# One instruction for both PSUM banks of an output block, other banks for the MLP's products, and later splits of the unmixed inner blocks

## The chip, the cores and the metric

The kernel runs on one core of a Trainium2 chip. The metric is the device time of one execution in microseconds (us), measured over several runs. TensorE (PE in the profile; PEld is its weight load) multiplies, VectorE (DVE), ScalarE (ACT) and GpSimd (POOL) compute elementwise, and SyncE (SP) issues most DMAs. PE writes only into PSUM, which has eight banks; each engine takes its instructions in order and waits on semaphores that other engines raise.

## The reference

One layer of a hybrid decoder on 544 tokens (512 of a prompt, 8 x 4 of samples), all in f32:

- `proj = rmsnorm(x) @ w_in`, cut into gated linear attention (GLA) and dilated attention with ALiBi; both are computed for prompt and samples, the samples with a key/value cache and a recurrent state.
- `x = x + concat(gla_part, att_part) @ w_out`
- `h = rmsnorm(x, ffn_norm_w)`; `x + square(relu(h @ w_up)) @ w_down`, with `w_up` 2048 x 8192 and `w_down` 8192 x 2048; then the final RMSNorm.
- Outputs are the two `y`, the prompt's and samples' keys and values, and the GLA states.

## The kernel before, in words

Everything lies transposed: 128 features on the partitions, 544 tokens along the free axis, in two halves of 272 (`HALF`). An f32 product is made of three: weights and activations are split into a high and a low part, and wh*xh, wh*xl and wl*xh are summed in PSUM. ACT copies the high part of a weight quad (128 x 512, `whP` in the MLP), DVE subtracts it from the weight to get the low part (`wlP`). Three buffers of each rotate (`NWH = 3`), and the splits are recorded ahead: before unit s of the MLP runs, units up to s+2 are split (`run`, line 1299, by `prep_to`). All engine calls go through one helper (line 95), so the profile's rows all carry L95 and are told apart by tile names.

**Projections** (to about 937 us of the profile). 48 blocks of `w_in` and then `w_out` are multiplied block by block over 24 x 2 matmuls a half; `mpair` (line 310) hands out the bank pairs 0,1 and 2,3 in turn, bank 0 and 2 for token half 0, bank 1 and 3 for half 1. `evac_in` (409), `evac_att` (1158) and `evac_wo` (1164) take the two halves out with one DVE instruction each. Attention and GLA steps are put between, by a planner that adds up estimated costs per engine, with banks 4 to 7.

**MLP, up** (about 937 to 1630 us). Pairs p = 0..31 of output blocks are computed with a seven-product scheme (Strassen's in Winograd's form): products P1 to P7 over sums of weight quads (`add_w`, DVE) and of activation halves. A unit is one product over four contraction blocks, 12 matmuls of 128 x 272. `ua`, `ub`, `uc` (1317) say which bank each product uses; `up_after` takes products out and forms the hidden block pair, `hidden_ops` squares, scales and stores it. Such small steps wait in the list `post`, of which `run` takes one before each unit. For p = 28 to 31 (g = 7) the hidden blocks are not mixed into sums: they are multiplied by the squared row norm (`mul`) and split into high and low (`spill_two`: an ACT copy, a DVE subtraction, two stores).

**MLP, down** (about 1630 to 2222 us). For g = 0..6 and p = 0..7, seven units in the order of `D_ORDER`. Each product is added into the accumulator tiles by one DVE instruction of 128 x 272 as soon as its unit ends (`down_after`; for g = 0 the first writes of four of the seven are ACT copies). Even p use banks 0 to 3, odd p banks 4 to 7 (lines 1510, 1516 and 1566):

```python
dbank = {"P1": (0, True), "P2": (0, False), "P5": (1, True), "P4": (1, False), "P7": (2, True), "P3": (2, False),
         "P6": (3, True)}
ps = halfb(bank[4 * (p % 2) + dbank[k][0]])
D_ORDER = ("P1", "P5", "P2", "P6", "P7", "P4", "P3")
```

**Last part** (2222 us to the end). The eighth group of `w_down` is multiplied directly, 16 blocks for each token half, two units a block, in the banks `LB` (1626); then the final norm.

Order within an engine is the order of the program text. Waits between engines are placed by the framework, which follows who wrote and read a tile.

Of the kernel before, what the change touches and what calls it, by code (L numbers as in the profile page):

```python
# [6 lines left out]
F32 = mybir.dt.float32  # L7
# [3 lines left out]
OP = mybir.AluOpType  # L11
AX = mybir.AxisListType

D = 2048
NTOK = 544
SEQ = 512
HALF = 272
# [105 lines left out]
def _body(ctx, nc, tc, A):  # L123
# [3 lines left out]
    psum = ctx.enter_context(tc.tile_pool(name="ps", bufs=1, space=bass.MemoryType.PSUM))  # L127
    ctx.enter_context(tc.manual_schedule())

    bank = [psum.tile([128, 512], F32, name=f"bank{i}") for i in range(8)]  # L130
    mbank = bank[:4]
    bfree = list(bank[4:])

# [60 lines left out]
    V, S, G, P = (Engine(e, k, clk) for e, k in ((nc.vector, "V"), (nc.scalar, "S"), (nc.gpsimd, "G"), (nc.tensor, "P")))  # L194
# [45 lines left out]
    i = 6  # L240
# [4 lines left out]

    def half(t, hf):
        return t[:, hf * HALF:(hf + 1) * HALF]

    def wops(i):
        return (lambda c: whm[i, c // 4][:, c % 4, :]), (lambda c: wlm[i, c // 4][:, c % 4, :])  # L250
# [8 lines left out]
    post = []  # L259
# [127 lines left out]
    r_bc = alloc()  # L387
# [9 lines left out]
    def rms_r(dst, srcs, n, banks):  # L397
        t, y = alloc(), alloc()
        for hf in range(2):
            for i, s in enumerate(srcs):  # L400
                P.matmul(banks[hf][:, :HALF], ones, half(s, hf), start=i == 0, stop=i == len(srcs) - 1)
        for hf in range(2):
            rsq(half(dst, hf), banks[hf][:, :HALF], n, half(t, hf), half(y, hf))
        rel(t, y)
# [4 lines left out]
    def evac_in(idx, pb):  # L409
        kind, h, _ = order[idx]  # L410
        t = alloc()
        sc = QSCALE if kind in ("q", "gq") else 1.0
        for hf in range(2):
            V.scalar_tensor_tensor(half(t, hf), pb[hf][:, :HALF], sc, half(r_bc, hf), op0=OP.mult, op1=OP.mult)
        B[kind, h] = t
        ready[kind, h] = slot[0]
        if kind in ("q", "k", "v"):
            j = "qkv".index(kind)
            S.activation(KVS[h // 4][:, j * 128 + (h % 4) * 32:j * 128 + (h % 4) * 32 + 32], t[:, SEQ:], AF.Copy)
        if kind in ("k", "v"):  # L420
            dst = A["kT" if kind == "k" else "vT"][h]
            defer(1, lambda: nc.sync.dma_start(dst, t))
# [625 lines left out]
    for idx in range(3, len(order)):  # L1048
# [3 lines left out]
        if kind == "gq" and h == 0:  # L1052
            begin()
            pb = mpair()
# [11 lines left out]
        pb = (b0, b1) if idx == 3 else mpair()  # L1066
# [90 lines left out]

    def evac_att(nb):
        def f(pb):
            for hf in range(2):  # L1160
                V.tensor_add(half(xr[nb], hf), pb[hf][:, :HALF], half(xr[nb], hf))
        return f

    def evac_wo(nb):
        def f(pb):
            t = xr[nb]
            for hf in range(2):
                V.tensor_add(half(t, hf), pb[hf][:, :HALF], half(t, hf))
            sq = {}

            def scaled():
                a = xa[nb] = alloc()
                S.activation(a, t, AF.Copy, scale=nw[:, 16 + nb:17 + nb])

            def squared():
                q = sq["q"] = ss2 if nb == 0 else alloc()
                S.activation(q, t, AF.Square)
                nc.gpsimd.dma_start(A["x2s"][nb], t)
                rel(t)

            def summed():
                if nb:
                    V.tensor_add(ss2, ss2, sq["q"])
                    rel(sq["q"])
            post.extend([scaled, squared, summed])
            j = nb - 8
            if j >= 0:
                post.extend(lambda f=f: f(j) for f in (up_b2, up_b1, up_ta, up_ta2, up_tb, up_tb2))
        return f
# [124 lines left out]
            unit_no[0] += 1  # L1314


    ua = [bank[0], bank[1]]
    ub, uc = [bank[2], bank[6]], [bank[3], bank[7]]
    tmp = {}
    hid = {}  # L1320

    def halfb(b):
        return b[:, :HALF]
# [2 lines left out]

    def r2_calc():
        r2sq = rr["sq"] = alloc()
        rms_r(r2sq, [ss2], D, (bank[4], bank[5]))
        V.tensor_mul(r2sq, r2sq, r2sq)  # L1330
        rel(ss2)

# [12 lines left out]
    def hidden_ops(p):  # L1345
        g, j = p // 4, p % 4
        a1, a2 = hid.pop((p, 0)), hid.pop((p, 1))
        if g == 7:
            def put(i, a):
                spill_two(a, A["hl"][2 * j + i], 0)  # L1350
                rel(a)
            post.extend([lambda: V.tensor_mul(a1, a1, rr["sq"]), lambda: V.tensor_mul(a2, a2, rr["sq"]),
                         lambda: put(0, a1), lambda: put(1, a2)])
            return
        dst = A["hs"][g, j]
        m = {}

        def mix_a():
            ta = m["a"] = alloc()
            V.tensor_sub(half(ta, 0), half(a1, 1), half(a1, 0))  # L1360
            V.tensor_sub(half(ta, 1), half(a1, 1), half(a2, 1))

        def first():
            t = alloc(R32)
            put_x(half(t, 0), half(t, 1), half(a1, 0))
            rel(a1)
            spill(t, dst[6])

        def mix_b():
            tb = m["b"] = alloc()  # L1370
            V.tensor_sub(half(tb, 0), half(a2, 1), half(m["a"], 0))
            V.tensor_sub(half(tb, 1), half(tb, 0), half(a2, 0))

        def put_a():
            spill_two(m["a"], dst, 2)
            rel(m["a"])

        def put_2():
            spill_two(a2, dst, 0)
            rel(a2)  # L1380

        def put_b():
            spill_two(m["b"], dst, 4)
            rel(m["b"])

        post.extend([mix_a, first, mix_b, put_a, put_2, put_b])
# [236 lines left out]
        return [kept, second, third]  # L1623

    perm = (0, 2, 4, 6, 1, 3, 5, 7)
    LB = [bank[i] for i in (0, 1, 2, 3)]
    fin = {}
    XL = {}

    def evac_last(hf, nb, pb):  # L1630
        t = half(acc[nb], hf)
        V.tensor_add(t, halfb(pb), t)
        if nb == 15:
            square(hf, nb)
# [50 lines left out]
    def last_mm(hf, nb, q):  # L1685
        def f():
            xs_ = XL.setdefault("x", [ah[n] for n in perm])
            key = ("L", hf, nb, q)
            ps = halfb(LB[nb % 4])
            for w, o in ((whm, 0), (whm, 1), (wlm, 0)):  # L1690
                for c in range(4):
                    P.matmul(ps, w[key][:, c, :], half(xs_[4 * q + c][o], hf), start=q == 0 and w is whm and o == 0 and c == 0,
                             stop=q == 1 and w is wlm and c == 3)
        return f
# [16 lines left out]
    for hf in range(2):  # L1711
        for nb in range(16):
            raw_seq.append((("l", hf, nb), A["wdn"][7, nb]))
            for q in range(2):
                raw_last["l", hf, nb] = len(units)

                def prep(hf=hf, nb=nb, q=q):
                    split_last(("L", hf, nb, q), mraw["l", hf, nb][:, 4 * q:4 * q + 4, :])
                add_unit(Unit(("L", hf, nb, q), prep, last_mm(hf, nb, q), before=last_before(hf, nb, q),
                              after=(lambda hf=hf, nb=nb: evac_last(hf, nb, LB[nb % 4])) if q else None))  # L1720


    xr_load(nbs[0])
# [203 lines left out]
```

## Time and profile before

| | |
|---|---|
| median of 3 runs | 2332.29 us (2331.51 to 2334.4) |
| profiled execution | 2335.45 us, span 2333.7 us |
| PE busy | 2294.7 us, 98% of the span, 18064 matmuls |
| DVE busy | 1992.2 us, 85%, 4079 instructions |
| ACT busy | 1127.8 us, 48% |
| granted TensorE clock | 0.997 on average |
| 12 matmuls of a unit in the down part | about 1.50 us |

A row of the timeline is: start, duration, engine, line, operation, out<-in, shape, number of instructions; in square brackets the idle time of the engine before it and what ended it. A row of the waits is: waiting engine and tile <- who was waited for: us in total, times, longest. A row of a window is its bounds, its length, the busy time of each engine with instruction counts, the granted clock, the DMA share and GB/s.

### The profile page before, as it was taken

The page shows a single profiled execution, that of the slowest core. Times are in us where ns is not written, and L with a number is a line of the kernel's source. Part 1 is how long each engine was busy: PE and PEld are TensorE (multiplying, and loading weights), DVE is VectorE, ACT ScalarE, POOL GpSimd, SP SyncE. Part 2 cuts the span into 40 slices and gives each one's busy share as a digit, 9 for nine tenths or more (in the row PEclk, how much of TensorE's full clock was granted, in tenths as well). Part 3 has the DMA queues.
Part 4 walks back from the last instruction along what each step waited for, and adds up shares of the span by engine and source line. Part 5 has one row for each costly group of instructions (what it writes and reads, how often), then busy time and mean ns, then how long its engine had stood idle before and what let it go on. Part 6 is the DMA issues. An engine that isn't in the chain of part 4 may idle for free.

```text
span 2333.7 us, 47577 instructions
## 1 busy us (share of the span) xinstructions
PE 2294.7 (98%) x18064; PEld 2262.4 (97%) x18064; DVE 1992.2 (85%) x4079; ACT 1127.8 (48%) x2129; POOL 397.8 (17%) x362
## 2 busy tenths in 40 slices
PE   8999999999999999999999999999999999999997
PEld 8999999999999999999999999999999999999997
DVE  6998987898887987889888888887788888888995
ACT  5333333333345345666666666665544444444465
POOL 3544553333444540000000000000000000000000
PEclk9999999999999999999999999999999999999999
DMA  6776865544625974365565566567754664664464
GB/s 239 255 264 246 293 223 206 175 171 158 243 79 181 336 274 170 116 194 179 188 208 189 175 195 208 179 205 247 274 181 162 220 207 147 223 216 157 169 213 150
DMA packets 168193, 473.46 MB, mean 203 GB/s; under 512 B 20091, under 2 KB 29307, under 8 KB 167964
## 3 DMA queue, kind: packets, MB, share of 16 engines
q1 hardware_dynamic: 157340, 439.67, 55.6%
q0 software_dynamic: 9472, 29.63, 3.6%
q8 instruction: 142, 2.33, 0.4%
q10 hardware_dynamic: 1152, 1.11, 0.1%
q14 instruction: 87, 0.71, 0.1%
HBM read 393.07 MB, written 77.27 MB: 202 GB/s over the span
## 4 chain that ended last, share of the span: by engine, by line
PE 83%; DVE 9%; DMA 4%; issue 2%; ACT 2%; POOL 0%; SPq 0%; DVEq 0%; ACTq 0%
PE bank L95 83%; DVE b L95 7%; DMA b<-vs 3%; DVE wlP L95 1%; ACT b L95 1%; DMA b<-hs 1%; ACT whP L95 0%; DVE AT L95 0%; DMA kv<-kcg 0%; DMA hs<-b 0%; DVE kv L95 0%; ACT wh L95 0%; DMA b<-xT 0%; DMA b<-wglr 0%; POOL gs L1214 0%
## 5 line engine op out<-in xcount | busy, mean ns | idle before, releaser
L95 PE MATMUL bank<-b,whP 128*128 128x272 f32 x6720 | 982.3, 288 | 5.8 <-ACT whP L95 3.0
L95 PEld LDWEIGHTS bank<-b,whP 128*128 128x128 f32 x6720 | 895.8, 188 | 9.8 <-ACT whP L95 6.1
L95 PE MATMUL bank<-b,wlP 128*128 128x272 f32 x3360 | 561.4, 289 | 2.2 <-DVE wlP L95 2.1
L95 PE MATMUL bank<-b,wh 128*128 128x272 f32 x3904 | 531.5, 289 | 2.8 <-ACT wh L95 2.6
L95 PEld LDWEIGHTS bank<-b,wh 128*128 128x128 f32 x3904 | 505.9, 188 | 4.7 <-ACT wh L95 4.5
L95 PEld LDWEIGHTS bank<-b,wlP 128*128 128x128 f32 x3360 | 473.5, 188 | 7.2 <-DVE wlP L95 3.5
L95 ACT ACTIVATE b<-b 128x544 fp32r<-128x544 f32 (+7 forms) x485 | 274.5, 571 | 267.2 <-DVE b L95 227.6
L95 ACT ACTIVATE whP<-b 128x512 fp32r<-128x512 f32 x480 | 300.7, 628 | 211.4 <-PE bank L95 131.1
L95 DVE TENSOR_TENSOR b<-b,b 128x272 f32<-128x272 f32 (+8 forms) x546 | 297.0, 559 | 56.5 <-ACT b L95 50.5
L95 DVE TENSOR_TENSOR wlP<-b,whP 128x512 fp32r<-128x512 f32 x480 | 327.8, 684 | 14.9 <-ACT whP L95 13.6
L95 POOL TENSOR_TENSOR wl<-raw,wh 128x512 fp32r<-128x512 f32 x180 | 271.8, 1515 | 383.0 <-ACT wh L95 324.6
L95 PE MATMUL bank<-b,wl 128*128 128x272 f32 x1952 | 298.5, 295 | 0.7 <-DVE wl L95 0.6
L95 POOL TENSOR_TENSOR b<-b,b 128x544 f32<-128x544 f32 (+2 forms) x26 | 36.4, 1403 | 1415.0 <-ACT b L95 1414.4
L95 PEld LDWEIGHTS bank<-b,wl 128*128 128x128 f32 x1952 | 261.7, 189 | 8.2 <-issue 3.9
L95 ACT ACTIVATE b<-bank 128x272 f32<-128x272 f32 (+5 forms) x243 | 96.9, 409 | 281.6 <-PE bank L95 256.1
L95 DVE TENSOR_TENSOR b<-b,bank 128x272 f32<-128x272 f32 x388 | 166.5, 432 | 59.8 <-PE bank L95 59.3
L95 ACT ACTIVATE wh<-raw 128x512 fp32r<-128x512 f32 x244 | 149.2, 622 | 131.0 <-PE bank L95 111.8
L95 DVE TENSOR_TENSOR wlP<-mraw,whP 128x512 fp32r<-128x512 f32 x206 | 140.4, 685 | 44.8 <-ACT whP L95 44.4
L95 ACT ACTIVATE whP<-mraw 128x512 fp32r<-128x512 f32 x206 | 126.7, 625 | 79.7 <-PE bank L95 76.0
L95 DVE SCALAR_TENSOR_TENSOR kv<-kv,b 128x320 f32<-128x320 f32 x256 | 160.7, 686 | 1.3 <-DMA kv<-vcg 1.1
L95 PE MATMUL bank<-b,b 128*128 128x272 f32 (+5 forms) x968 | 143.4, 304 | 6.2 <-ACT b L95 6.2
L95 DVE TENSOR_TENSOR wlP<-raw,whP 128x512 fp32r<-128x512 f32 x154 | 105.2, 685 | 34.2 <-ACT whP L95 34.2
(89 smaller groups left out, 1805.3 us busy)
## 6 DMA issues: line engine op xcount, KB each, us to landing
hs<-b SPq DMA_DIRECT2D x196, 272.0 KB, 6.0
b<-hs SPq DMA_DIRECT2D x196, 272.0 KB, 5.0
raw<-win SPq DMA_DIRECT2D x90, 512.0 KB, 4.7
mraw<-wdn SPq DMA_DIRECT2D x82, 512.0 KB, 4.0
kv<-kcg SPq DMA_DIRECT2D x64, 640.0 KB, 5.0
kv<-vcg SPq DMA_DIRECT2D x64, 640.0 KB, 5.0
mraw<-wup SPq DMA_DIRECT2D x74, 512.0 KB, 4.4
raw<-wdn SPq DMA_DIRECT2D x62, 512.0 KB, 3.8
```

What stands on the lines that cost most here:

```text
L95: return f(*a, **k)
```

## The change

Banks 0,1 and banks 2,3 become one tile each of [128, 2, 512] (`duo`), and `bank[0]` to `bank[3]` are views of them. `evac_in`, `evac_att` and `evac_wo` take both halves out with one DVE instruction of 128 x 544, except for the blocks that are not in such a pair. The MLP's up part gets other banks (`ua` 4 and 5, `ub` 0 and 2, `uc` 6 and 7; the norm there 6 and 7), the last part two banks in turn in place of four. The down part's table is as it was. In `hidden_ops` two empty steps stand between the scaling and the splits of the unmixed blocks.

```diff
-    bank = [psum.tile([128, 512], F32, name=f"bank{i}") for i in range(8)]
+    duo = [psum.tile([128, 2, 512], F32, name=f"bank{2 * i}") for i in range(2)]
+    bank = [duo[i // 2][:, i % 2, :] for i in range(4)]
+    bank += [psum.tile([128, 512], F32, name=f"bank{i}") for i in range(4, 8)]
...
+    def halves(t):
+        return t.rearrange("p (a n) -> p a n", a=2)
+
+    def both(pb):
+
+        return duo[0 if pb[0] is mbank[0] else 1][:, :, :HALF]
...
-        for hf in range(2):
-            V.scalar_tensor_tensor(half(t, hf), pb[hf][:, :HALF], sc, half(r_bc, hf), op0=OP.mult, op1=OP.mult)
+        if any(pb[0] is m for m in mbank):
+            V.scalar_tensor_tensor(halves(t), both(pb), sc, halves(r_bc), op0=OP.mult, op1=OP.mult)
+        else:
+            for hf in range(2):
+                V.scalar_tensor_tensor(half(t, hf), pb[hf][:, :HALF], sc, half(r_bc, hf), op0=OP.mult, op1=OP.mult)
...
-            for hf in range(2):
-                V.tensor_add(half(t, hf), pb[hf][:, :HALF], half(t, hf))
+            V.tensor_add(halves(t), both(pb), halves(t))
...
-    ua = [bank[0], bank[1]]
-    ub, uc = [bank[2], bank[6]], [bank[3], bank[7]]
+    ua, ub, uc = [bank[4], bank[5]], [bank[0], bank[2]], [bank[6], bank[7]]
...
-        rms_r(r2sq, [ss2], D, (bank[4], bank[5]))
+        rms_r(r2sq, [ss2], D, (bank[6], bank[7]))
...
-            post.extend([lambda: V.tensor_mul(a1, a1, rr["sq"]), lambda: V.tensor_mul(a2, a2, rr["sq"]),
-                         lambda: put(0, a1), lambda: put(1, a2)])
+            post.extend([lambda: V.tensor_mul(a1, a1, rr["sq"]), lambda: V.tensor_mul(a2, a2, rr["sq"]), lambda: None,
+                         lambda: put(0, a1), lambda: None, lambda: put(1, a2)])
...
-    LB = [bank[i] for i in (0, 1, 2, 3)]
+    LB = [bank[0], bank[2]]
...
-            ps = halfb(LB[nb % 4])
+            ps = halfb(LB[nb % 2])
```

**PE in the down part**, group g = 3, pair p = 2 (even, so banks 0 to 3): the first matmul of each unit, with the semaphores it waits for. In a name such as whP5_3_2 stand product, g and p; the number behind is a buffer's. Before:

```order
L95 MATMUL bank0_66<-b1342_22819,whP1_3_2_24030 128x272 [waits Activation_49]
...
L95 MATMUL bank1_67<-b1348_22901,whP5_3_2_24051 128x272 [waits Activation_49]
...
L95 MATMUL bank0_66<-b1360_23067,whP2_3_2_24072 128x272 [waits DVE_49,Activation_49]
...
L95 MATMUL bank3_69<-b1373_23233,whP6_3_2_24093 128x272 [waits Activation_49]
...
L95 MATMUL bank2_68<-b1348_22901,whP7_3_2_24114 128x272 [waits Activation_49]
...
L95 MATMUL bank1_67<-b1373_23233,whP4_3_2_24133 128x272 [waits Activation_49]
```

and now (bank0_66 and bank2_67 are the two double tiles):

```order
L95 MATMUL bank0_66<-b1342_22739,whP1_3_2_23950 128x272 [waits Activation_49]
...
L95 MATMUL bank0_66<-b1348_22821,whP5_3_2_23971 128x272 [waits DVE_49,Activation_49]
...
L95 MATMUL bank0_66<-b1360_22987,whP2_3_2_23992 128x272 [waits DVE_49,Activation_49]
...
L95 MATMUL bank2_67<-b1373_23153,whP6_3_2_24013 128x272 [waits Activation_49]
...
L95 MATMUL bank2_67<-b1348_22821,whP7_3_2_24034 128x272 [waits DVE_49,Activation_49]
...
L95 MATMUL bank0_66<-b1373_23153,whP4_3_2_24053 128x272 [waits Activation_49]
```

No matmul moves. The first of P5 and the first of P7 now also wait for DVE; that of P2 did before too. What each waits for on DVE, by the semaphore's value: P5 for the DVE instruction that takes P1 out, P2 for the one that takes P5 out (before: P1), P7 for the one that takes P6 out. In each case that is the unit directly ahead.

**PE at the start of the up part**: the last matmuls of the projections (weights wl127) and the first of the MLP. Before:

```order
L95 MATMUL bank0_66<-b374_9204,wl127_1_10947 128x272
L95 MATMUL bank1_67<-b374_9204,wl127_1_10947 128x272
L95 MATMUL bank2_68<-b385_10042,whP2_0_0_10990 128x272 [waits DVE_49,Activation_49]
L95 MATMUL bank2_68<-b398_10195,whP2_0_0_10990 128x272
L95 MATMUL bank2_68<-b411_10348,whP2_0_0_10990 128x272
```

and now:

```order
L95 MATMUL bank0_66<-b371_9065,wl127_1_10869 128x272 x2
L95 MATMUL bank0_66<-b374_9148,wl127_1_10869 128x272 x2
L95 MATMUL bank0_66<-b385_9976,whP2_0_0_10911 128x272 [waits DVE_49,Activation_49]
L95 MATMUL bank0_66<-b398_10127,whP2_0_0_10911 128x272
L95 MATMUL bank0_66<-b411_10278,whP2_0_0_10911 128x272
```

The first product of the MLP now goes into the tile that the last projection block has just filled, so its DVE wait is for that block's evacuation.

**DVE in the up part**, p = 29, where the hidden blocks of p = 28 (b1101 and b1116) are scaled by b520 and split. Before:

```order
L95 TENSOR_TENSOR b1101_19341<-b1101_19341,b520_11621 128x544
...
L95 TENSOR_TENSOR b1116_19517<-b1116_19517,b520_11621 128x544
L95 TENSOR_TENSOR b1128_19660<-b1123_19616,raw_116_19144 128x512 [waits DVE_49]
L95 TENSOR_TENSOR wlP6_29_1_19663<-b1123_19616,whP6_29_1_19662 128x512 [waits PE_49,Activation_49]
L95 TENSOR_TENSOR b1130_19667<-b1101_19341,b1129_19666 128x544 [waits DMAHW2_49,DVE_49,Activation_49]
L95 TENSOR_TENSOR b1133_19688<-raw_117_19146,raw_118_19260 128x512 [waits DVE_49]
L95 TENSOR_TENSOR wlP3_29_0_19691<-b1127_19641,whP3_29_0_19690 128x512 [waits PE_49,Activation_49]
L95 TENSOR_TENSOR b1135_19695<-b1116_19517,b1134_19694 128x544 [waits Activation_49]
```

and now:

```order
L95 TENSOR_TENSOR b1116_19437<-b1116_19437,b520_11541 128x544
L95 TENSOR_TENSOR b1128_19580<-b1123_19536,raw_116_19064 128x512 [waits DVE_49]
L95 TENSOR_TENSOR wlP6_29_1_19583<-b1123_19536,whP6_29_1_19582 128x512 [waits PE_49,Activation_49]
L95 TENSOR_TENSOR b1131_19604<-raw_117_19066,raw_118_19180 128x512 [waits DVE_49]
L95 TENSOR_TENSOR wlP3_29_0_19607<-b1127_19561,whP3_29_0_19606 128x512 [waits PE_49,Activation_49]
L95 TENSOR_TENSOR b1133_19611<-b1101_19261,b1132_19610 128x544 [waits DVE_49,Activation_49]
...
L95 TENSOR_TENSOR wlP7_29_0_19653<-b1131_19604,whP7_29_0_19652 128x512 [waits PE_49,Activation_49]
L95 TENSOR_TENSOR b1138_19657<-b1116_19437,b1137_19656 128x544 [waits Activation_49]
```

The first split's subtraction comes one unit later, the second's two, behind the low part of P7's first quad.

More of the change, by code (lines that the diff above doesn't have):

```diff
@@ L1159, in f @@
         def f(pb):
-            for hf in range(2):
-                V.tensor_add(half(xr[nb], hf), pb[hf][:, :HALF], half(xr[nb], hf))
+            V.tensor_add(halves(xr[nb]), both(pb), halves(xr[nb]))
         return f
@@ L1166, in f @@
             t = xr[nb]
-            for hf in range(2):
-                V.tensor_add(half(t, hf), pb[hf][:, :HALF], half(t, hf))
+            V.tensor_add(halves(t), both(pb), halves(t))
             sq = {}
@@ L1719, in _body @@
                 add_unit(Unit(("L", hf, nb, q), prep, last_mm(hf, nb, q), before=last_before(hf, nb, q),
-                              after=(lambda hf=hf, nb=nb: evac_last(hf, nb, LB[nb % 4])) if q else None))
+                              after=(lambda hf=hf, nb=nb: evac_last(hf, nb, LB[nb % 2])) if q else None))
     xr_load(nbs[0])
```

## The prediction

> **What bounds the kernel now.** I read the page's busy times, then the chain of waits in order of time, then the stretches of the span, then the groups of DVE instructions by shape. From these views, in that order:
>
> ```profile
> PE 2294.7 (98%) x18064; PEld 2262.4 (97%) x18064; DVE 1992.2 (85%) x4079; ACT 1127.8 (48%) x2129; POOL 397.8 (17%) x362
> ...
> 1636.50 683.30 PE bank L95 x5437
> ...
> 1800.00:2100.00 300.00, 300.00 (x2394) 300.00 (x2393) 265.65 (x514) 126.38 (x200) 0.00 (x0) 1.00 0.59 200
> ...
> L95 DVE TENSOR_TENSOR b<-b,bank 128x272 f32<-128x272 f32 x388 | 166.5, 432 | 59.8 <-PE bank L95 59.3 <-ACT b L95 0.5
> ```
>
> PE sets the end. From 1636.5 us to 2319.8 us, nearly all of the down part and all of the last, the chain is PE alone, 5437 matmuls without a gap. In 1800 to 2100 us PE is busy 300 of 300 us and DVE 265.65 (89%). So nothing taken off DVE there can shorten the span, while any time that PE is made to wait lengthens it one for one. The fourth row is the instruction that takes a product out in the down part: 432 ns. DVE's idle time ahead of it is nearly all waiting for PE (59.3 of 59.8 us): the product is late for DVE, not DVE for the product.
>
> **The change, part by part.**
>
> *New waits in the down part.* Banks 0 and 1 are now one tile, banks 2 and 3 another, and the framework's waits follow tiles. For even p the order of the products is P1 (bank 0), P5 (1), P2 (0), P6 (3), P7 (2), P4 (1), P3 (2). Three units now write into a tile whose other half DVE must still empty of the unit directly ahead: P5 after P1, P2 after P5, P7 after P6. The order of the changed program shows each of the three with that DVE wait. P4 waits for P2's evacuation and P3 for P7's, with two units and one unit between, so those cost nothing. Odd p lies in banks 4 to 7 and is as before. That makes 3 waits x 4 even p x 7 groups = 84.
>
> What one costs comes from the timeline of PE and DVE, one even or odd p being like the other in it before:
>
> ```profile
> 1906.16 0.68 DVE L95 TENSOR_TENSOR b<-raw,raw 128x512 f32<-128x512 f32 x1
> ...
> 1907.01 1.18 PE L95 MATMUL bank<-b,whP 128*128 128x272 f32 x8
> 1907.36 0.43 DVE L95 TENSOR_TENSOR b<-b,bank 128x272 f32<-128x272 f32 x1
> 1907.71 0.68 DVE L95 TENSOR_TENSOR b<-b,raw 128x512 f32<-128x512 f32 x1
> ...
> 1908.31 0.68 DVE L95 TENSOR_TENSOR wlP<-b,whP 128x512 fp32r<-128x512 f32 x1
> ...
> 1908.53 1.18 PE L95 MATMUL bank<-b,whP 128*128 128x272 f32 x8
> 1908.91 0.43 DVE L95 TENSOR_TENSOR b<-b,bank 128x272 f32<-128x272 f32 x1
> ...
> 1910.05 1.17 PE L95 MATMUL bank<-b,whP 128*128 128x272 f32 x8
> 1910.25 0.44 DVE L95 TENSOR_TENSOR b<-b,bank 128x272 f32<-128x272 f32 x1 [0.31 <-PE bank L95]
> ...
> 1911.56 1.16 PE L95 MATMUL bank<-b,whP 128*128 128x272 f32 x8
> 1911.76 0.44 DVE L95 TENSOR_TENSOR b<-b,bank 128x272 f32<-128x272 f32 x1 [0.47 <-PE bank L95]
> ```
>
> The sum of two raw quads (1906.16) prepares P2 and stands right behind P3's evacuation, so the next evacuation, 1907.36, is P1's; then come P5's (1908.91), P2's and P6's (1911.76). The PE rows between are the starts of P5, P2, P6 and P7, 1.50 us apart. P1's evacuation starts 0.35 us after P5 began (1907.36 - 1907.01), P6's 0.20 us after P7 began, the lag of a DVE that was idle. P5's lag, 0.38, is DVE's backlog of two sums; once PE has paused for P1, DVE is through with P6's split at about 1907.01 + 1.98 and P5 ends at about + 2.5, so 0.20 holds there too. Then 0.43 us of the instruction. What lies between its end and PE's flow I take from the nearest row of the same kind: P4 after P7 at the very end of the up part, where the same bank is used by adjacent units.
>
> ```profile
> 1625.51 0.66 PE L95 MATMUL bank<-b,wlP 128*128 128x272 f32 x4
> ...
> 1626.45 0.43 DVE L95 TENSOR_TENSOR b<-bank,b 128x272 f32<-128x272 f32 x1
> ...
> 1627.00 1.05 PEld L95 LDWEIGHTS bank<-b,whP 128*128 128x128 f32 x8 [1.06 <-ACT whP L95]
> 1627.03 1.24 PE L95 MATMUL bank<-b,whP 128*128 128x272 f32 x8 [0.86 <-DVE b L95]
> ```
>
> DVE ends at 1626.88, PE's row starts at 1627.03 and lasts 1.24 in place of 1.17: 0.15 + 0.07 = 0.22 us. The lower bound is 0.05, a bare release without the slower restart (DVE to PE at 1576 us, below). So:
>
> - P1 to P5: 0.35 + 0.43 + 0.22 = 1.00 us
> - P5 to P2 and P6 to P7: 0.20 + 0.43 + 0.22 = 0.85 us each
> - an even p: 2.70 us; 28 of them: **75.6 us**
> - bounds: all three at 0.20 + 0.43 + 0.05 = 0.68 us, 57.1 us; P1 and P5 at the lag 0.38, 2 x 1.03 + 0.85 = 2.91 us, 81.5 us.
>
> Nothing can hide this: PE has no other unit to run, since its instructions stand in order, and it had no slack. Behind the waiting matmul stand only PE's own; DVE and ACT gain time.
>
> The Trainium skill, "PSUM — Partial Sum Buffer", section "PSUM bank collisions raise a hardware error", asks only that one bank be guarded, within a group of 32 partitions. The rows agree that two banks go in parallel: at 1907.36 DVE empties bank 0 while PE fills bank 1. By that rule alone the 84 waits would be needless and the sum here 0; but it is the program's waits that run.
>
> *The start of the up part.* The MLP's first product now goes into the tile that the last projection block has filled.
>
> ```profile
> 936.55 1.18 PE L95 MATMUL bank<-b,wl 128*128 128x272 f32 x8
> ...
> 937.56 1.17 PE L95 MATMUL bank<-b,whP 128*128 128x272 f32 x8
> ...
> 938.28 0.78 DVE L95 TENSOR_TENSOR b<-bank,b 128x272 f32<-128x272 f32 x2
> ...
> 948.84 1.76 PE L95 MATMUL bank<-b,whP 128*128 128x272 f32 x8 [0.55 <-ACT whP L95]
> ...
> 954.42 0.39 PE L95 MATMUL bank<-b,whP 128*128 128x272 f32 x1 [0.72 <-DVE b L95]
> ```
>
> That evacuation starts at 938.28; as one instruction about 0.72 us, with 0.22 behind it, it would let PE start at 939.22 in place of 937.56: 1.7 us. PE loses some 1.9 us anyway between 948.84 and 954.42, waiting for operands that DVE and ACT make from the same evacuation (0.55 + 0.59 of slow matmuls + 0.72 are in the rows). So the bounds are 0 and 1.7; the splits wait in part for PE's progress, so I take 1.0.
>
> *Later splits at the end of the up part.* PE stalls there nine times for p = 29 to 31; the first and the last of them with what stands ahead of the first:
>
> ```profile
> 1573.45 0.66 ACT L95 ACTIVATE b<-b 128x544 fp32r<-128x544 f32 x1 [2.77 <-DVE wlP L95]
> ...
> 1574.14 0.72 DVE L95 TENSOR_TENSOR b<-b,b 128x544 fp32r<-128x544 f32 x1 [0.73 <-ACT b L95]
> 1574.68 1.27 PE L95 MATMUL bank<-b,whP 128*128 128x272 f32 x8 [0.45 <-ACT whP L95]
> ...
> 1575.51 0.69 DVE L95 TENSOR_TENSOR wlP<-b,whP 128x512 fp32r<-128x512 f32 x1
> ...
> 1576.25 0.77 PE L95 MATMUL bank<-b,wlP 128*128 128x272 f32 x4 [0.30 <-DVE wlP L95]
> ...
> 1622.40 0.77 PE L95 MATMUL bank<-b,wlP 128*128 128x272 f32 x4 [0.17 <-DVE wlP L95]
> ```
>
> DVE waits 0.73 us for the copy of the second hidden block, and P3's weights come late behind it. A stall costs the idle time in brackets (2.85 us over the nine) and 0.1 us of restart: 3.8 us. The change puts this split behind the first split of P7, where no sums are due. It can give all of it back or, where the next stall takes its place, nothing: I take 2.5 us. Four spills to memory come a unit or two later; they are read hundreds of us on.
>
> *One evacuation instead of two.* 46 blocks of `w_in` and 32 of `w_out`. Issues of 272 stand 0.35 us apart and of 512 0.60 (1907.36, 1907.71, 1908.31), so 1.04 ns an element, 0.63 for 544 against 0.70: 78 x 0.07 = 5.5 us less on DVE. In the projections PE has few stalls:
>
> ```profile
> 30.00:600.00 570.00, 562.78 (x4421) 546.81 (x4420) 491.13 (x1219) 195.11 (x432) 252.87 (x166) 1.00 0.62 219
> ```
>
> 7.2 us in 570, in GLA's chains of DVE and ACT, which do not contain the evacuations. Worth 0, at best a fraction of these; if the cover went, it would cost a tenth of a microsecond a block.
>
> *Two banks in the last part.* A block's bank comes again after one block in place of three.
>
> ```profile
> L95 PE MATMUL bank<-b,whL x512: 282/288/490, 2222.3 to 2319.0; 128*128 128x272 f32 x171
> ...
> 2251.12 0.43 DVE L95 TENSOR_TENSOR b<-bank,b 128x272 f32<-128x272 f32 x1
> ```
>
> A block takes (2319.6 - 2222.3) / 32 = 3.04 us; the ninth ends at about 2249.6 and its evacuation, the latest of the part, at 2251.55, so with 0.22 for the release 0.9 us before PE comes to that bank again. Cost 0.
>
> Sum: 75.6 + 1.0 - 2.5 = **+74 us**. The profiled execution would go from 2335.45 us (span 2333.7) to about 2409.5; the median lies 3.2 us below the profiled time, so against 2332.29 I predict **2406 us**.
>
> **Rivals.**
>
> *PE's clock falls.* Short pauses every few units could lower the granted clock.
>
> ```profile
> 1612.00:1640.00 28.00, 25.59 (x194) 24.41 (x194) 23.28 (x40) 16.57 (x31) 0.00 (x0) 1.00 0.90 304
> ...
> 2300.00:2334.00 34.00, 20.97 (x162) 20.11 (x161) 12.56 (x31) 14.98 (x30) 2.91 (x4) 0.87 0.22 74
> ```
>
> With 9% of pauses of up to 1.2 us it stays at 1.00; at 0.87 it is only where PE stops for good. Even p's work is 28 x 10.5 = 294 us; at 0.87 it would take 44 us more: 2450 us. Chance 0.04. The Trainium skill, "TensorE: Matmul & The Clock Gate", section "A second HAM failure mode: psum-queue depth-cycling", tells of just such short idling between PSUM banks making the gate swing to half speed; by it the same work would cost up to 294 us more. The window at 1612 does not bear that out.
>
> *DVE becomes late as well.* If every evacuation came to stand behind one more split (0.60 us), 84 x 0.60 = 50 us more: 2456 us. Against it: per two p DVE has 36 instructions, 22 of 0.60 and 14 of 0.35, 18 us, and PE now gives it 23.7. Chance 0.05.
>
> *The release is quicker than any row.* Only the instruction itself counts, 84 x 0.43 = 36 us: 2367 us. For it speaks nothing but that modelled ends may be late. Chance 0.04.
>
> *The waits are met when PE comes, so that only the gain of the later splits remains:* 2332.3 - 3.8 = 2328 us, not slower. It decides if evacuations end before the next unit starts; every row above has them start 0.20 us or more after it. Chance 0.02.
>
> **How the numbers follow.** Forecast 0.85, rivals 0.04, 0.05, 0.04, 0.02. The forecast's own bounds are 2332.3 + 57.1 - 3.8 = 2386 and 2332.3 + 81.5 + 1.7 = 2416; I give 2385 to 2420, for lags that the pauses themselves shift. The dearer and cheaper cases stay outside. A change under 0.2% (4.7 us) can't be told from none here; the last rival lies at that edge, so faster 0.01, same 0.01, slower 0.98.
>
> **What would show it.** In the changed profile: PE waits for DVE's `b` in the down part some 84 times, 0.6 to 0.8 us of idle each, three per even p and none in odd p; PE's busy share there falls to about 89%, with the clock still 1.00; the nine stalls at the end of the up part are fewer; DVE has 78 fewer instructions. It is wrong if the units of even p follow each other at 1.50 us, if odd p slow down too, or if the clock in that stretch is below 1.00.

## The result and the profile after

The changed kernel takes **2407.03 us** (median of 6 runs, 2404.76 to 2412.85) against 2332.89 us (six runs, 2331.51 to 2334.4) for the kernel before: ratio **1.032, 95% interval 1.0307 to 1.0334**. It is 3.2% slower, 74 to 75 us. The profiled execution took 2404.76 us with a span of 2403.0 us; the granted clock was 0.998 on average.

First the busy times and three groups of instructions of the changed kernel (after the bar: busy us, mean ns of one, then the idle time of the engine ahead of them and who ended it):

```profile
PE 2308.9 (96%) x18064; PEld 2263.9 (94%) x18064; DVE 1990.2 (83%) x4001; ACT 1127.7 (47%) x2129; POOL 397.8 (17%) x362
...
L95 PE MATMUL bank<-b,whP 128*128 128x272 f32 x6720 | 986.9, 289 | 60.9 <-DVE b L95 50.6 <-ACT whP L95 8.2 <-ACT b L95 1.9
...
L95 DVE TENSOR_TENSOR b<-b,bank 128x272 f32<-128x272 f32 x388 | 167.4, 434 | 127.0 <-PE bank L95 126.4
...
L95 DVE SCALAR_TENSOR_TENSOR b<-bank,b 128x544 f32<-128x544 f32 x46 | 33.1, 720 | 27.0 <-PE bank L95 26.9
```

The first of these groups in the kernel before:

```profile
L95 PE MATMUL bank<-b,whP 128*128 128x272 f32 x6720 | 982.3, 288 | 5.8 <-ACT whP L95 3.0 <-DVE b L95 1.6 <-DMA b<-hs 1.0
```

A matmul with MLP weights takes 289 ns (288 before) and the DVE instruction that takes a product out 434 ns (432 before). What changed is idle time: PE now stands 60.9 us ahead of such matmuls (5.8 before), of which DVE's `b` ends 50.6, and DVE stands 127.0 us ahead of its evacuations where it stood 59.8. The two engines take turns: PE waits for DVE, and then DVE for PE. DVE has 78 instructions fewer.

Next the waits of PE in the changed kernel (us in total, times, longest):

```profile
PE bank L95 <- DVE b L95: 59.4, 82, 2.1
PE bank L95 <- ACT b L95: 10.1, 7, 6.3
PE bank L95 <- ACT whP L95: 8.2, 14, 0.8
```

The first of them in the kernel before:

```profile
PE bank L95 <- DVE b L95: 9.9, 13, 1.8
```

Row by row, PE's timeline from 1623 us to the end of the down part has exactly 84 pauses: 68 put down to DVE's `b`, 12 to ACT's `whP` and 4 to ACT's `b`. Those named `whP` are P5 and P2 of the first pair in each of the groups 1 to 6. There too PE starts 0.10 us after the evacuation ahead has ended, while the split of the weights had ended 0.35 to 0.53 us before, so they are waits for the evacuation like the others. The four named `b` of ACT stand in group 0, where ACT takes P1 out.

The busy share in the middle of the down part, the same stretch that was shown of before (bounds, length, busy time of PE, PEld, DVE, ACT and POOL, clock, DMA share, GB/s):

```profile
1800.00:2100.00 300.00, 275.95 (x2137) 269.08 (x2136) 237.52 (x457) 112.58 (x178) 0.00 (x0) 1.00 0.50 169
```

PE is busy 275.95 of 300 us at a clock of 1.00. And a whole even p with the beginning of the next one, from the timeline (start, duration, engine, line, operation; in brackets the idle time before it and who ended it):

```profile
1933.08 1.16 PE L95 MATMUL bank<-b,whP 128*128 128x272 f32 x8
...
1934.95 0.43 DVE L95 TENSOR_TENSOR b<-b,bank 128x272 f32<-128x272 f32 x1
...
1935.53 1.23 PE L95 MATMUL bank<-b,whP 128*128 128x272 f32 x8 [0.78 <-DVE b L95]
...
1937.29 0.44 DVE L95 TENSOR_TENSOR b<-b,bank 128x272 f32<-128x272 f32 x1 [0.71 <-PE bank L95]
...
1937.88 1.24 PE L95 MATMUL bank<-b,whP 128*128 128x272 f32 x8 [0.62 <-DVE b L95]
...
1939.45 1.17 PE L95 MATMUL bank<-b,whP 128*128 128x272 f32 x8
...
1941.16 0.44 DVE L95 TENSOR_TENSOR b<-b,bank 128x272 f32<-128x272 f32 x1 [0.47 <-PE bank L95]
...
1941.75 1.24 PE L95 MATMUL bank<-b,whP 128*128 128x272 f32 x8 [0.62 <-DVE b L95]
...
1959.30 1.25 PE L95 MATMUL bank<-b,whP 128*128 128x272 f32 x8 [0.78 <-DVE b L95]
```

The PE rows are the starts of P1, P5, P2, P6 and P7, and the last one P5 of the next even p. P5 would start 1.50 us after P1, at 1934.58; it starts at 1935.53, when the evacuation of P1 (1934.95 to 1935.38) is over. P2 waits in the same way for P5's and P7 for P6's; P6 does not wait. From P7 to the next P5, eleven units with all of the odd p among them, 17.55 us pass; less the 1.01 us of that P5's wait this is 1.50 us a unit, so odd p are as before: 10.53 us for seven units, 10.5 to 10.6 before. Two p, from P5 to P5 (1935.53 to 1959.30), take 23.77 us, so the even one 23.77 - 10.53 = 13.24, which is 2.71 more than an odd one.

Where the difference of the two profiled executions arose, by rows at the same places of both programs:

| place | before | after | change on the way |
|---|---|---|---|
| last unit of the projections starts | 936.55 | 933.60 | -2.95 |
| first product of the MLP starts | 937.56 | 936.26 | +1.65 |
| PE row at the end of the loss of operands | 954.42 | 951.48 | -1.64 |
| wait for `wlP` behind it | 986.87 | 984.38 | +0.45 |
| P4 of p = 31 | 1627.03 | 1622.48 | -2.06 |
| first `whL` of the last part | 2222.3 | 2291.9 | +74.15 |
| span | 2333.7 | 2403.0 | -0.3 |

These two executions lie only 69.3 us apart and the medians 74: the profiled execution of before, 2335.45 us, is slower than all six of its measured runs, that of the changed kernel the fastest of its six.

### The profile page after: what moved, and what is told of

It reads as the page before. It is cut to its first block, busy times and chain, and to the rows that moved or that the text cites. A ratio compares the mean times of both kernels' runs of the same rounds, so it can differ in the third digit from the quotient of the medians.

```text
span 2403.0 us, 47554 instructions
## 1 busy us (share of the span) xinstructions
PE 2308.9 (96%) x18064; PEld 2263.9 (94%) x18064; DVE 1990.2 (83%) x4001; ACT 1127.7 (47%) x2129; POOL 397.8 (17%) x362
## 4 chain that ended last, share of the span: by engine, by line
PE 80%; DVE 12%; DMA 3%; issue 3%; ACT 2%; POOL 0%; SPq 0%; DVEq 0%; ACTq 0%
PE bank L95 80%; DVE b L95 9%; DMA b<-vs 3%; DVE wlP L95 2%; ACT b L95 1%; ACT whP L95 1%; DVE AT L95 0%; DMA kv<-kcg 0%; DVE kv L95 0%; ACT wh L95 0%; DMA raw<-wdn 0%; DMA b<-xT 0%; DMA b<-wglr 0%; DMA b<-hs 0%; POOL gs L1224 0%
## 5 line engine op out<-in xcount | busy, mean ns | idle before, releaser
L95 PE MATMUL bank<-b,whP 128*128 128x272 f32 x6720 | 986.9, 289 | 60.9 <-DVE b L95 50.6
L95 DVE TENSOR_TENSOR b<-b,bank 128x272 f32<-128x272 f32 x388 | 167.4, 434 | 127.0 <-PE bank L95 126.4
```

The lines of the kernel that those rows point to most:

```text
L95: return f(*a, **k)
```

## The experiments

All ratios are against the kernel before, measured beside it on the same chip. 0.1% is 2.3 us. The kernel before took 2333.63 us beside the first four kernels, 2331.95 beside the next four and 2334.34 beside the last two.

**Is it the sharing of a tile by adjacent units?** The table of the down part is changed so that P5 and P4 lie in bank 2, P7 and P3 in bank 1. The double tiles and everything else of the change stay.

```diff
-    dbank = {"P1": (0, True), "P2": (0, False), "P5": (1, True), "P4": (1, False), "P7": (2, True), "P3": (2, False),
+    dbank = {"P1": (0, True), "P2": (0, False), "P5": (2, True), "P4": (2, False), "P7": (1, True), "P3": (1, False),
```

> The changed kernel with one table altered: in the down part P5 and P4 use bank 2, P7 and P3 bank 1, so that units next to each other never share a double tile; everything else as changed. Theory (the 84 waits for the unit directly ahead are the whole loss): they are gone, the down part takes 590 us again in place of 664, and what is left is the gain ahead of it in the changed trace, 4.5 us: about 2328 us (2325 to 2332). Rival (double tiles cost as such, by DVE reading one half while PE writes the other, or by the other banks): stays above 2390 us.

Measured: 2333.06 us (2330.74 to 2336.95), ratio 0.9999, interval 0.999 to 1.0008. The same stretch of this kernel:

```profile
1800.00:2100.00 300.00, 300.00 (x2397) 300.00 (x2396) 265.20 (x513) 126.56 (x200) 0.00 (x0) 1.00 0.60 204
```

PE is busy 300 of 300 us again. The whole loss hangs on which two units share a tile: 1.032 against 0.9999, some 75 us. But this kernel is not faster than before, though I had expected it to be (2325 to 2332 us): I had counted on 4.5 us gained ahead of the down part, of which the two profiles owed 2.95 to the projections. In the changed kernel and four others of this study whose projections are the same instructions, the first product of the MLP starts at 936.3, 936.3, 937.7, 939.2 and 939.5 us, so those 2.95 us were no gain but lie within what one execution differs from another there. Part of that is the granted clock: in 668 to 673 us it is 1.00 in the two early executions and 0.66 in the three late ones, and in 318 to 322 us it is 0.57 in the profile of before and 1.00 in that of the changed kernel.

**The wait at the start of the up part.** As above, and the two banks of `ub` are exchanged, so that the MLP's first product lies in the other double tile.

```diff
-    ua, ub, uc = [bank[4], bank[5]], [bank[0], bank[2]], [bank[6], bank[7]]
+    ua, ub, uc = [bank[4], bank[5]], [bank[2], bank[0]], [bank[6], bank[7]]
```

> The same, and the two banks of ub exchanged, so that the MLP's first product goes into bank 2 and not into the tile that the last projection block has just filled. Theory: the start wait (1.5 us idle at 936 us of the changed trace) vanishes, but 1.2 us of it was made up later by shorter waits, so 0.5 us less than with the table alone, about 2327.5 us. Rival (the start wait costs in full): 1.7 us less, about 2326.5 us.

Measured: 2331.95 us (2328.87 to 2340.47), ratio 0.9995, interval 0.9984 to 1.0006: 1.1 us below the kernel above, and the two intervals overlap. The traces say more than the times. The start of the changed kernel, and of this one:

```profile
935.40 0.72 DVE L95 TENSOR_TENSOR b<-bank,b 128x544 f32<-128x544 f32 x1
...
936.26 1.24 PE L95 MATMUL bank<-b,whP 128*128 128x272 f32 x8 [1.49 <-DVE b L95]
...
951.48 0.39 PE L95 MATMUL bank<-b,whP 128*128 128x272 f32 x1 [0.54 <-DVE b L95]
```

```profile
943.93 1.75 PE L95 MATMUL bank<-b,whP 128*128 128x272 f32 x8 [0.55 <-ACT whP L95]
949.51 0.40 PE L95 MATMUL bank<-b,whP 128*128 128x272 f32 x1 [0.72 <-DVE b L95]
```

With the wait (first rows) PE loses 1.49 us at once, and the stall for `whP` with the slow matmuls behind it, which the second rows have, is absent. In the table above the +1.65 is followed by -1.64: by 951.48 us nothing of the start wait is left.

**The empty steps alone.** The kernel before with only the two empty steps in `hidden_ops`.

```diff
-            post.extend([lambda: V.tensor_mul(a1, a1, rr["sq"]), lambda: V.tensor_mul(a2, a2, rr["sq"]),
-                         lambda: put(0, a1), lambda: put(1, a2)])
+            post.extend([lambda: V.tensor_mul(a1, a1, rr["sq"]), lambda: V.tensor_mul(a2, a2, rr["sq"]), lambda: None,
+                         lambda: put(0, a1), lambda: None, lambda: put(1, a2)])
```

> The kernel before with nothing but the two empty steps between scaling and splits of the unmixed hidden blocks. Theory: of the nine stalls at the end of the up part (3.8 us with restarts) some remain, so 1.5 to 3.8 us less than before, about 2330.5 us. Rival (the stalls only move): 2332.9 us, no change.

Measured: 2329.92 us (2328.29 to 2337.28), ratio 0.9984, interval 0.9974 to 0.9995: 3.7 us faster. Its PE pauses between 1570 and 1629 us that the timeline marks (those above 0.15 us):

```profile
1574.53 1.27 PE L95 MATMUL bank<-b,whP 128*128 128x272 f32 x8 [0.19 <-ACT whP L95]
1594.43 0.77 PE L95 MATMUL bank<-b,wlP 128*128 128x272 f32 x4 [0.29 <-DVE wlP L95]
1595.43 1.27 PE L95 MATMUL bank<-b,whP 128*128 128x272 f32 x8 [0.23 <-ACT whP L95]
1621.66 1.23 PE L95 MATMUL bank<-b,whP 128*128 128x272 f32 x8 [1.49 <-DVE b L95]
```

Of nine such stalls three are left, and two more of 0.13 and 0.14 us lie just under the mark; but P4 at the very end now waits 1.49 us in place of 0.86: part of the gain goes into the next wait. From the `wlP` wait at 983.50 us to that P4 this kernel needs 638.16 us, the one before 640.16 (986.87 to 1627.03): 2.0 us. The changed kernel needs 638.10 for it.

**Single tiles.** The changed kernel with eight tiles of one bank again and two evacuations a block (that part of the change is not shown); the banks of the up part, two banks in the last part and the empty steps stay.

```diff
-    duo = [psum.tile([128, 2, 512], F32, name=f"bank{2 * i}") for i in range(2)]
-    bank = [duo[i // 2][:, i % 2, :] for i in range(4)]
-    bank += [psum.tile([128, 512], F32, name=f"bank{i}") for i in range(4, 8)]
+    bank = [psum.tile([128, 512], F32, name=f"bank{i}") for i in range(8)]
```

> The changed kernel without the double tiles: eight single banks and two evacuations a block as before, but the new banks of the up part, the two banks of the last part and the empty steps. Theory: no wait for the unit directly ahead in the down part, so no loss; the gain of the steps alone, about 2330.5 us (2328 to 2333). If the single evacuation is worth the 3 us that the projections gained in the changed trace, this kernel lies 3 us above the one with the table. Rival (the other banks cost): above 2390 us.

Measured: 2329.63 us (2326.39 to 2330.92), ratio 0.9982, interval 0.9973 to 0.9992. This is the fastest kernel of the study: 4.2 us below the kernel before, and with no line of the down part touched. The empty steps alone gave 3.7 of them; the other banks and the two banks of the last part add nothing that can be told.

**Is the loss in proportion to the waits?** The new table for groups 0 to 2 only, the changed kernel's table for groups 3 to 6: 48 adjacent pairs in place of 84. The place where the product is computed takes the same choice (not shown).

```diff
+    dperm = dict(dbank, P5=(2, True), P4=(2, False), P7=(1, True), P3=(1, False))
...
-        ps = halfb(bank[4 * (p % 2) + dbank[k][0]])
+        ps = halfb(bank[4 * (p % 2) + (dperm if g < 3 else dbank)[k][0]])
```

> The changed kernel with the conflict-free table for g = 0 to 2 alone; g = 3 to 6 keep the 48 waits. Theory (each wait costs the same, wherever it stands): 4 groups x 4 even p x 2.70 us = 43 us above the kernel with the table throughout, about 2371 us. Rival (the first waits are dear and later ones hide behind them, or the loss is one of the whole part): not in proportion, nearer to 2407 or to 2330 us.

Measured: 2375.88 us (2374.64 to 2377.65), ratio 1.0189, interval 1.0174 to 1.0205. Against 0.9999 without adjacent pairs that is 44.3 us for 48 waits, 0.92 us each; the other 36 then make 30.6 us, 0.85 each. The intervals alone (4 to 5 us on each sum) don't tell 0.92 from 0.85, but the trace of the changed kernel has two sources for such a difference. In group 0 some of the first evacuations are ACT copies, and two p take 23.48 us (P7 to P7, 1633.95 to 1657.43) in place of 23.77. And in group 6 P5 waits 1.49 us in three of four even p:

```profile
2220.29 0.43 DVE L95 TENSOR_TENSOR b<-b 128x272 f32<-128x272 f32 x1
2220.64 0.44 DVE L95 TENSOR_TENSOR b<-b,b 128x272 f32<-128x272 f32 x1
2221.00 0.43 DVE L95 TENSOR_TENSOR b<-b,bank 128x272 f32<-128x272 f32 x1
...
2221.57 1.23 PE L95 MATMUL bank<-b,whP 128*128 128x272 f32 x8 [1.49 <-DVE b L95]
```

Two instructions that finish accumulators (a subtraction and a scaling, `finish_acc`) stand ahead of P1's evacuation there, 0.71 us: work on DVE that was free while PE did not wait for DVE now costs its full length.

**Is it these three pairs, or any adjacent pair?** The banks are dealt out so that three other pairs share a tile: P6 after P2, P4 after P7 and P3 after P4; P1, P5 and P2 no longer do.

```diff
-    dbank = {"P1": (0, True), "P2": (0, False), "P5": (1, True), "P4": (1, False), "P7": (2, True), "P3": (2, False),
-             "P6": (3, True)}
+    dbank = {"P1": (0, True), "P2": (0, False), "P5": (2, True), "P4": (2, False), "P7": (3, True), "P3": (3, False),
+             "P6": (1, True)}
```

> The changed kernel with a third table: P5 and P4 in bank 2, P7 and P3 in bank 3, P6 in bank 1. Now three other units follow a neighbour in the same double tile: P6 after P2, P4 after P7, P3 after P4. Theory: lags of 0.20, 0.20 and 0.26 us, the instruction 0.43 and the release 0.22: 0.85 + 0.85 + 0.91 = 2.61 us an even p, 28 x 2.61 = 73 us, about 2401 us. Rival (the price belongs to P5, P2 and P7, whose weights are sums): well below, about 2330 to 2370 us.

Measured: 2406.41 us (2405.41 to 2408.93), ratio 1.0321, interval 1.0306 to 1.0337: as slow as the changed kernel, and 5 us above what I had expected. In groups 1 to 5 of its trace an even p takes 13.0 to 13.1 us where an odd one takes 10.5: 2.6 us for three waits, as expected (2.61). In group 6 P6 waits three times as long in three of four even p: DVE has accumulators to finish there and comes late to P2's evacuation. Behind the third of these pauses the granted clock is down for a while:

```profile
2226.12 1.24 PE L95 MATMUL bank<-b,whP 128*128 128x272 f32 x8 [1.83 <-DVE b L95]
...
2276.19 1.77 PE L95 MATMUL bank<-b,whP 128*128 128x272 f32 x8 [1.81 <-DVE b L95]
...
2276.00:2280.00 4.00, 3.81 (x18) 3.84 (x19) 1.69 (x4) 0.63 (x1) 0.00 (x0) 0.58 0.40 132
```

So the price belongs to no particular products: any adjacent pair pays lag, instruction and release. How long the lag is depends on what DVE has to do just then, and that this table and the first one add up to the same time within 1 us is chance.

**The same rule in the up part.** The new table in the down part, and the old banks in the up part (`ua` 0 and 1, `ub` 2 and 6, `uc` 3 and 7): in the up part P1 then follows P4 in one tile 31 times, and P5 another product 16 times. The norm has its old banks 4 and 5 too; these and the down part's table are not shown.

```diff
-    ua, ub, uc = [bank[4], bank[5]], [bank[0], bank[2]], [bank[6], bank[7]]
+    ua = [bank[0], bank[1]]
+    ub, uc = [bank[2], bank[6]], [bank[3], bank[7]]
```

> The changed kernel with the conflict-free table in the down part, but the banks of before in the up part (ua 0 and 1, ub 2 and 6, uc 3 and 7). Now P1 follows P4 of the pair before in one double tile (31 times, taken out by ACT in 0.40 us), and for even p P5 writes beside the bank that DVE adds P1's sum from (16 times, ACT copy and DVE add in a row). Theory: 31 x (0.20 + 0.40 + 0.22) + 16 x (0.20 + 0.40 + 0.43 + 0.27) = 25 + 21 = 46 us above the kernel with the table, about 2374 us. Rival (the up part, where ACT and DVE have more slack, hides them): about 2330 us.

Measured: 2374.96 us (2371.69 to 2378.57), ratio 1.019, interval 1.0173 to 1.0207: 44.6 us above the kernel with the new table, where I had expected 46. Its PE waits:

```profile
PE bank L95 <- DVE b L95: 33.2, 32, 4.1
PE bank L95 <- ACT b L95: 24.5, 36, 6.2
```

Now ACT's `b` is waited for 36 times (the kernel with the new table: 3), since P4 of the up part is taken out by ACT. So the loss is bound neither to DVE nor to the down part. It also shows what the other banks in the up part are there for: with double tiles and the old ones, that part would lose too.

**The price of one wait.** In the changed kernel, the evacuations on which PE waits (P1, P5 and P6 of even p in groups 1 to 6, 72 in all) are done in two instructions, each adding half of the product.

```diff
+            if g and p % 2 == 0 and k in ("P1", "P5", "P6"):
+                for _ in range(2):
+                    V.scalar_tensor_tensor(dst, ps, -0.5 if k == "P1" else 0.5, dst, op0=OP.mult, op1=OP.add)
+            else:
+                add_acc(dst, ps, g == 0 and k in ("P1", "P2", "P3", "P4"), k == "P1")
```

> The changed kernel, with the evacuations that PE waits for made twice as long: for g from 1 on and even p, P1, P5 and P6 are added in two DVE instructions of half the value each (same result but for rounding). Theory (PE waits for the end of the evacuation): each of the 72 waits is longer by the distance of two such instructions, 0.35 us: 25 us more, about 2432 us. Rival (the wait is set by something else, for example the readiness of the split weights): no more than a few us above 2407 us.

Measured: 2442.3 us (2440.24 to 2444.11), ratio 1.0473, interval 1.0458 to 1.0489: 35 us above the changed kernel where I had expected 25. The trace has why:

```profile
1977.39 0.92 DVE L95 SCALAR_TENSOR_TENSOR b<-bank,b 128x272 f32<-128x272 f32 x2 [0.73 <-PE bank L95]
...
1978.45 1.24 PE L95 MATMUL bank<-b,whP 128*128 128x272 f32 x8 [1.10 <-DVE b L95]
```

The pair takes 0.92 us, not 0.43 + 0.35. Each instruction alone lasts 0.44, and the second starts at 1977.87, 0.48 us behind the first and 0.03 after its end: it reads what the first has written. It is not the kind of instruction: the same kind and shape, also out of PSUM but on two different blocks, takes 0.78 us for two in the kernel before, so 0.35 apart:

```profile
71.10 0.78 DVE L95 SCALAR_TENSOR_TENSOR b<-bank,b 128x272 f32<-128x272 f32 x2
```

PE's pause goes from 0.62 to 1.10, by 0.48, and 72 x 0.48 = 34.6 us is the 35 that was measured (to some 5 us). In the rows it holds more closely: each of the groups 1 to 5 is 5.6 to 5.8 us longer than in the changed kernel, 0.47 to 0.48 for each of its 12 waits. Group 6 is 8.3 us longer; behind a pause of 1.97 us its granted clock is down as well:

```profile
2280.00:2286.00 6.00, 4.90 (x22) 4.61 (x22) 3.02 (x7) 1.11 (x2) 0.00 (x0) 0.50 0.25 87
```

So a wait here costs what stands on DVE between the unit's end and the release.

**What one instruction for two banks is worth.** Double tiles and one evacuation a block, no adjacent pairs, and the empty steps taken out again. The new table and the exchanged banks of `ub`, which this kernel and the next have too, are not shown.

```diff
-            post.extend([lambda: V.tensor_mul(a1, a1, rr["sq"]), lambda: V.tensor_mul(a2, a2, rr["sq"]), lambda: None,
-                         lambda: put(0, a1), lambda: None, lambda: put(1, a2)])
+            post.extend([lambda: V.tensor_mul(a1, a1, rr["sq"]), lambda: V.tensor_mul(a2, a2, rr["sq"]),
+                         lambda: put(0, a1), lambda: put(1, a2)])
```

> Double tiles and one evacuation of 544 for two of 272, with no unit next to another in the same tile and without the two empty steps; the rest as in the changed kernel. Theory: the single evacuation is worth nothing and only the empty steps gained, so this is the kernel before: ratio 1.000, about 2332 to 2334 us. Rival 1, it saves the 5.5 us that it takes off DVE: ratio 0.9977, about 2327.5 us. Rival 2, it costs the 2.3 us by which the run with everything but the adjacent waits was above the one with single tiles: ratio 1.001, about 2335.5 us.

Measured: 2336.71 us (2332.33 to 2345.64), ratio 1.0015, interval 1.0003 to 1.0027. It saves nothing; this kernel is some 3 us slower than before (0.7 to 6.3).

And the same double tiles with two evacuations a block, with the empty steps (one of three places shown; `evac_in` and `evac_wo` are changed likewise):

```diff
-            V.tensor_add(halves(xr[nb]), both(pb), halves(xr[nb]))
+            for hf in range(2):
+                V.tensor_add(half(xr[nb], hf), pb[hf][:, :HALF], half(xr[nb], hf))
```

> Double tiles, no unit next to another in the same tile, with the empty steps, but every block taken out by two instructions of 272 as before. Theory (a tile of two banks costs only where adjacent units share it): the gain of the empty steps alone, ratio 0.9984, about 2329.3 us, no different from single tiles. Rival, the wider waits cost something in the projections too, where a block's first half is no longer released by itself: about the ratio 0.9995 of the run with one instruction, 2332 us.

Measured: 2332.28 us (2330.03 to 2336.35), ratio 0.9993, interval 0.9985 to 1.0001. The kernel of "The wait at the start of the up part" differs from this one only in that it takes a block out with one instruction, and it has 0.9995 (0.9984 to 1.0006): two instructions or one make no difference that can be told. Both lie above single tiles (0.9982). So it is the double tile that costs, not the longer instruction, and the traces show where. Group 6 of the down part takes 87.1 us in all five kernels with double tiles and the new table there, whether with one evacuation or with two, and 84.9 in the three with single tiles. In this kernel and in the one with single tiles, P6 of an even p of group 6:

```profile
2183.46 0.79 DVE L95 TENSOR_TENSOR b<-b,b 128x272 f32<-128x272 f32 x2
2184.17 0.43 DVE L95 TENSOR_TENSOR b<-b,bank 128x272 f32<-128x272 f32 x1
...
2184.74 1.25 PE L95 MATMUL bank<-b,whP 128*128 128x272 f32 x8 [0.52 <-DVE b L95]
```

```profile
2175.57 1.17 PE L95 MATMUL bank<-b,whP 128*128 128x272 f32 x8
2175.66 0.43 DVE L95 TENSOR_TENSOR b<-b,bank 128x272 f32<-128x272 f32 x1
```

With single tiles P6 starts before P5 has been taken out. With double tiles and the new table P5 lies in P6's tile with one unit, P2, between them, and that is not enough here: the two instructions at 2183.46 finish accumulators, P5's evacuation comes behind them, and P6 waits for it. That happens in three even p and makes 2.2 us, which accounts for most of the 2 to 3 us. I had taken it that a tile of two banks costs only where adjacent units share it; that is so only while DVE is less than a unit late.

## Why the prediction was right, and where not

*The new waits* (75.6 us predicted): right in kind and in size. There are 84, three per even p and none in odd p. Their terms hold one by one. P1's evacuation starts 0.37 us after P5 should have begun (0.35 taken), P5's and P6's 0.19 and 0.21 (0.20 taken, on the argument that DVE's backlog of sums is gone once PE has paused); the instruction takes 0.43; the release 0.15, and the first eight matmuls 1.23 to 1.24 us in place of 1.16 to 1.17, which is the 0.07 of restart. An even p costs 2.71 us by PE's starts, 2.70 predicted. The down part grew by 74.15 us between the two profiles, and by 74.9 in the times (1.032 against 0.9999 with the new table). What the sum left out are two opposite things of a few microseconds: group 0, where it is cheaper, and three waits of group 6, 0.71 us dearer each. The latter is the rival "DVE late too", in 3 of 84 places. One of the signs was off: PE's busy share in 1800 to 2100 us is 92%, not 89%. The 89% sets the whole delay, 2.7 us in 23.7, against the span. But the matmul rows overlap (1.16 and 0.66 us in a unit of 1.50), so the tail of the last row ahead of a pause counts as busy; the idle time, 0.6 to 0.8 us a pause as predicted, gives 92%.

*The start of the up part* (+1.0, bounds 0 to 1.7): the wait itself was 1.65 us, as the upper bound had it, but all of it was covered by operands that come late anyway; the lower bound was right. Mis-sized by 1.0.

*The later splits* (-2.5): 2.0 to 2.06 us in the rows, 3.7 in the times (interval 1.2 to 6.1). Six of nine stalls went, and P4 of p = 31 took back 0.63.

*One evacuation in place of two* (0): right, no gain, though DVE has less to do (0.9995 with one instruction, 0.9993 with two).

*Two banks in the last part* (0): it takes from 2291.9 to the end as long as before, to 0.3 us, and the kernel with single tiles, which has them, is the fastest.

Together, by the times: the kernel with single tiles, which has the rest of the change but for the single evacuation, is 4.2 us faster than before (2.5 predicted for the later splits). From there to the changed kernel it is 1.032 against 0.9982, 78.9 us (predicted: 75.6, and 1.0 for the start). Each of these is known to 2 to 4 us. The two errors, 1.7 and 2.3 us, have opposite signs; that the total of +74 is met within 1 us is in part luck.

*The rivals.* In the changed kernel the clock did not fall: with a pause of 0.5 to 1.5 us every few microseconds the granted clock is 1.00 between 1628 and 2292 us. But the reading behind that rival, that the clock is lower only where PE stops for good, was wrong. In the profile of before it is 0.57 in 318 to 322 us, behind a pause of 1.80 us (and the longest pause in the window at 1612 is 0.97 us, not 1.2). In the down part of two experiments it fell once each, behind pauses of 1.81 and 1.97 us. In each of these two, two other pauses of the same length passed without a fall, so length alone does not decide it, and what does was not found. The Trainium skill, "TensorE: Matmul & The Clock Gate", section "A second HAM failure mode: psum-queue depth-cycling", tells of another kernel whose frequent short idling between PSUM banks made the gate swing; the trace of the changed kernel does not show that for its pauses. That the release would be quicker than any row is excluded by the pause of 0.62 us at P2 and P7 alone, longer than the instruction's 0.44. And no wait was met when PE came.

## What to carry to other kernels

When several PSUM banks become one tile, look for consecutive units that write into it: the framework's wait then holds the whole tile until the other bank has been emptied, and each such pair costs lag, evacuation and release on the matmul engine, here 0.9 us. It costs almost nothing where the order of banks keeps the pairs apart, so deal out the banks by the order of the units, and do that everywhere the banks are used, not only where the double tile is wanted. One unit between them is enough only while the evacuating engine is less than a unit late: in group 6, where it was later, 2.2 us were lost even so. Taking work off an engine that is itself waiting gained nothing here. A pause in the engine that sets the end makes the others' spare work count, as the two instructions ahead of an evacuation in group 6 show.

## What the runs showed of the hardware

- Two DVE instructions of 128 x 272 that both read PSUM start 0.48 us apart if the second needs what the first wrote (1977.39 and 1977.87). Independent ones of the same kind and shape start 0.35 us apart. I had priced the doubled evacuation with the latter.
- PE's first eight matmuls after a pause of 0.5 to 1.5 us take 1.22 to 1.27 us in place of 1.15 to 1.18, at a clock of 1.00; a longer pause does not make them slower.
- In single executions the granted clock is halved for a few microseconds behind a PE pause of about 2 us (0.50 in 2280 to 2286 us of the kernel with doubled evacuations), and after other pauses of that length it is not.
- The same instructions of the projections end up to 3.2 us apart in five executions (first product of the MLP from 936.3 to 939.5 us). A gain of 3 us between two single traces in that part is no evidence.
